# Hybrid DeltaNet and window-attention layer, one core: SiLU gate on ACT, decays computed one supertile ahead, another PSUM split, triangle DMAs in four pieces

## Chip, cores and metric

The kernel runs on one core of a Trainium2 chip. The metric is the device time of one execution in microseconds (us); smaller is better. Engines are named as in the profile: PE multiplies matrices, DVE, ACT and POOL work on vectors, SP issues most DMAs. Each engine takes its instructions strictly in the order in which they were written into its stream.

## What is computed

One layer of a decoder step for a prompt of 4096 tokens (width 1024) and 8 single-token samples. Float32 throughout in the reference:

```python
h = x * (1 + scale) + shift
proj = h @ w_in
qkv, new_conv = causal_conv(conv_buf, proj[..., 0:1536], conv_w)      # 4 taps, then silu
qa = l2_normalize(qa) * 128 ** -0.5 ; ka = l2_normalize(ka)           # 4 heads of 128
beta = sigmoid(proj_beta)
g = -exp(a_log) * softplus(proj_decay + dt_bias)
# gated delta rule: S_t = exp(g_t) (I - b_t k_t k_t^T) S_{t-1} + b_t k_t v_t^T ; o_t = S_t^T q_t
oa = rms_norm(o, norm_a) * silu(za)
ob = window_attention(rotary(qb), rotary(kb), vb, sinks) * silu(zb)   # window 128
y = layer_norm(alpha * x + (1 + gate) * (concat(oa, ob) @ w_out))
```

Outputs are y for prompt and samples and the new convolution, delta and window states.

## The kernel before

The program has three stages. Stage 1 (to about 1200 us) computes the delta-rule branch for the prompt and, piece by piece, side work (weight splits for later stages, the samples' delta step). Stage 2 (to about 1600 us) is the window attention. Stage 3 is the gate and output projections with layer norm. The change touches stage 1 only, and of the later stages nothing.

Stage 1 loops over 16 **supertiles** `s` of 256 tokens, each two chunks `c` of 128, four heads each, so eight (chunk, head) pairs `m`. A supertile passes through:

- `xt`: modulated input `hT` in two float16 halves, written by ACT (L253, L255) and DVE (L256). It is made one supertile ahead, by `ahead()` in the middle of `front`.
- `front`, decays: eight small projections into `bd`, then beta (Tanh, L273) and `g` by `softplus_ops` (an Exp and a chain of DVE instructions, L105), split into `g16`. Later in `front` PE sums `g16` along the chunk (`tr<-g,c`, `pga<-c,g`), and ACT takes exponentials: `G` (L333), the 128x128 decay matrices `dec` (L348), the last column `eGl` (L349).
- `front`, `group`: channels of keys, queries and values, 24 matmuls of 128x256 for each 128 channels (`pj<-hT,w`), an eviction (`u`, L309, and L313), three more convolution taps on DVE (L315), then the gate. With `th = tanh(x/2)` from ACT (L321) DVE forms `(th+1)*x` (L322), which is twice SiLU. L2 norms, `Kd`, `Vn` and the constants 4e-6 and 0.25 allow for that factor.
- `front`, products: keys, queries and values are transposed through a PSUM bank called `tr` (L355, L389, L399). `pga<-kqv` gives k.k and q.k; DVE makes the triangular `U` (L379) and `Aqk` (L382).
- `lanes`: the eight 128x128 triangles' four diagonal 32x32 blocks are inverted on DVE. `U`'s blocks go to DRAM (L411, four DMAs), come back as `LU` (one DMA that repeats the 128 KB four times along the partitions), 31 steps of two DVE instructions each (L420, L422) build `LV`, which goes to DRAM in one DMA (L424) and comes back as `VTd` in four (L429).
- `gdn_inv`: from `VTd` and `U16` the whole inverse, for each chunk a chain PE, ACT, DVE, PE with small operands (L433 to L480). `gdn_c`: the recurrence through the state `S` (L491 `r`, L503 `ut`, L508 `S`).

PSUM has eight banks: `pga` 1, `xt` 1, `tr` 1, `pj` 2, `pgi` 3. The `xt` bank serves the side work.

The order in which each engine takes its work is set when the program is built: a scheduler of the tile framework moves instructions of different steps and supertiles between each other. So the inverse of one supertile lies between the products of the next, and the 62 steps on `LV` lie between convolution taps.

```python
LU = w1p.tile([128, 32, 32], F32, name="LU", bufs=1)
sp.dma_start(LU.rearrange("p a b -> p (a b)"), d1[None].to_broadcast([4, 32, 1024]))
...
d2w = d2.rearrange("l (j c i) -> c l j i", c=4, i=32)
sp.dma_start(d2w, LV)
```

Of the kernel before, what the change touches and what calls it, by code (L numbers as in the profile page):

```python
# [9 lines left out]
F32 = mybir.dt.float32  # L10
# [23 lines left out]
def body(ctx, tc, I, O, seq):  # L34
# [5 lines left out]
    def mm(out, l, r, st=True, sp_=True):  # L40
        pe.matmul(out, l, r, start=st, stop=sp_)  # L41
# [69 lines left out]
    with ExitStack() as p1:  # L111
# [5 lines left out]
        wk = p1.enter_context(tc.tile_pool(name="wk", bufs=2))  # L117
        sml = p1.enter_context(tc.tile_pool(name="sml", bufs=2))
        pga = p1.enter_context(tc.tile_pool(name="pga", bufs=1, space=PSUM))
        pxt = p1.enter_context(tc.tile_pool(name="pxt", bufs=1, space=PSUM))  # L120
        pst = p1.enter_context(tc.tile_pool(name="pst", bufs=1, space=PSUM))
        pj = p1.enter_context(tc.tile_pool(name="pj", bufs=2, space=PSUM))
        pgi = p1.enter_context(tc.tile_pool(name="pgi", bufs=3, space=PSUM))

        def tr_ps(shape, dt=F32):
            return pst.tile(shape, dt, name="tr")

        def xt_ps(shape, dt=F32):
            return pxt.tile(shape, dt, name="xt")

        def load_x(s):

            xs = []
            for q in range(2):
                x = wf.tile([128, 4, 256], F32, name="x", bufs=3)
                sp.dma_start(x, I["xT"][s][:, 4 * q:4 * q + 4])
                xs.append(x)
            return xs
# [88 lines left out]
        def load_bd():  # L227
            sp.dma_start(wbd32, I["wbd"])
            split(wbd[:, :, 0:8], wbd[:, :, 8:16], wbd32)
# [27 lines left out]
            sp.dma_start(hD[s], hT.rearrange("p a k t -> p (a k t)"))  # L257
            return hT

        def front(s, hT, ahead):  # L260

            bd = tr_ps([128, 2, 16])
            for c in range(2):
# [5 lines left out]
            act.activation(bdS, bd, AF.Copy, scale=IWS)  # L269
            x8 = sml.tile([128, 2, 8], F32, name="x8")  # L270
            dve.tensor_add(x8, bdS[:, :, 0:8], bdS[:, :, 8:16])
            be = sml.tile([128, 2, 4], F32, name="be")
            act.activation(be, x8[:, :, 0:4], AF.Tanh, scale=0.5)  # L273
            dve.tensor_scalar(be, be, 1.0, 0.5, op0=ALU.add, op1=ALU.mult)
            xd = sml.tile([128, 2, 4], F32, name="xd")
# [2 lines left out]
            softplus_ops(sml, xd, g, [128, 2, 4], "sp")  # L278
            dve.tensor_mul(g, g, nega[:, None, :].to_broadcast([128, 2, 4]))
            dve.tensor_scalar(g, g, -30000.0, None, op0=ALU.max)  # L280
            g16 = sml.tile([128, 2, 8], F16, name="g16")
            gf = g.rearrange("p a b -> p (a b)")
            dve.tensor_copy(g16[:, 0], gf)
            dve.tensor_sub(g16[:, 1], gf, g16[:, 0])
            kqv = wk.tile([128, 8, 256], F32, name="kqv", bufs=2)
            vv = wf.tile([128, 4, 256], F32, name="vv", bufs=1)
            U = wk.tile([128, 8, 128], F32, name="U", bufs=1)
# [2 lines left out]
            Kd = wk.tile([128, 8, 128], F32, name="Kd", bufs=2)  # L290
            Vn = wk.tile([128, 8, 128], F32, name="Vn", bufs=2)
            sse = sml.tile([128, 2, 8], F32, name="sse")
            sc = sml.tile([128, 6, 8], F32, name="sc")
            junk = wf.tile([128, 128], F32, name="junk", bufs=1)

            def group(grp, dst):
                for pr in range(2):
                    b0 = grp * 4 + pr * 2
                    u = wf.tile([128, 2, 259], F32, name="u", bufs=3)
                    pool.tensor_copy(u[:, :, 0:3], hist[:, b0:b0 + 2, :])  # L300
                    ps = pj.tile([128, 2, 256], F32, name="pj")
                    for b2 in range(2):
                        n = 0
                        w = w1[b0 + b2]
                        for k in range(8):
                            for wi, hi in ((0, 0), (0, 1), (1, 0)):
                                mm(ps[:, b2, :], w[:, wi, k, :], hT[:, hi, k, :], n == 0, n == 23)
                                n += 1
                    act.activation(u[:, :, 3:259], ps, AF.Copy, scale=IWS)  # L309
                    for b2 in range(2):  # L310
                        blk = b0 + b2
                        d = dst[:, pr * 2 + b2, :]
                        act.activation(d, ps[:, b2, :], AF.Copy, scale=cw64[:, blk:blk + 1])  # L313
                        for j in range(3):
                            dve.scalar_tensor_tensor(d, u[:, b2, j:j + 256], cwj(j, blk), d,  # L315
                                                     op0=ALU.mult, op1=ALU.add)
                    pool.tensor_copy(hist[:, b0:b0 + 2, :], u[:, :, 256:259])
                    if pr == 0:
                        yield
                th = wf.tile([128, 4, 256], F32, name="th", bufs=1)  # L320
                act.activation(th, dst, AF.Tanh, scale=0.5)  # L321
                dve.scalar_tensor_tensor(dst, th, 1.0, dst, op0=ALU.add, op1=ALU.mult)  # L322


            keys, qrs, vls = group(1, kqv[:, 4:8]), group(0, kqv[:, 0:4]), group(2, vv)
            next(keys)
            next(keys, None)
            next(qrs)
            ps = tr_ps([128, 8])
            mm(ps, triU, g16[:, 0], True, False)  # L330
            mm(ps, triU, g16[:, 1], False, True)
            G = sml.tile([128, 4, 8], F32, name="G")
            act.activation(G[:, 0], ps, AF.Exp)  # L333
            act.activation(G[:, 1], ps, AF.Copy, scale=-1.0)
            dve.tensor_scalar(G[:, 2], G[:, 0], -1.0, None, op0=ALU.mult)
            eGl = sml.tile([128, 2, 4], F32, name="eGl")
            decs = []
            for c in range(2):
                dec = wf.tile([128, 4, 128], F32, name="dec", bufs=2)
                pg = pga.tile([128, 4, 128], F32, name="pga")  # L340
                for h in range(4):
                    m = 4 * c + h
                    mm(pg[:, h, :], idb, negm, True, False)
                    mm(pg[:, h, :], g16[:, 0, m:m + 1].to_broadcast([128, 128]), triU, False, False)
                    mm(pg[:, h, :], g16[:, 1, m:m + 1].to_broadcast([128, 128]), triU, False, True)
                for h in range(4):
                    m = 4 * c + h
                    act.activation(dec[:, h, :], pg[:, h, :], AF.Exp, bias=G[:, 1, m:m + 1])  # L348
                act.activation(eGl[:, c, :], pg[:, :, 127], AF.Exp)  # L349
                decs.append(dec)  # L350

            for c in range(2):
                pk = tr_ps([128, 4, 128])
                for h in range(4):
# [1 line left out]
                for h in range(4):  # L356
                    m = 4 * c + h
                    act.activation(junk, pk[:, h, :], AF.Square, accum_out=sse[:, 1, m:m + 1])
                    act.activation(Kd[:, m, :], pk[:, h, :], AF.Copy, scale=decs[c][:, h, 127:128])
            dve.tensor_scalar(sse[:, 1], sse[:, 1], 4e-6, None, op0=ALU.add)  # L360
            dve.tensor_scalar(sc[:, 5], sse[:, 1], 0.25, None, op0=ALU.mult)
            pool.tensor_tensor(sc[:, 0], sc[:, 5], half_pos[:, 0:8], op=ALU.pow)
            dve.reciprocal(sc[:, 1], sse[:, 1])
            dve.tensor_mul(sc[:, 2], be.rearrange("p a b -> p (a b)"), sc[:, 1])
            dve.tensor_scalar(sc[:, 3], sc[:, 2], -1.0, None, op0=ALU.mult)
# [20 lines left out]
            for c in range(2):  # L386
# [3 lines left out]
                for h in range(4):  # L390
                    m = 4 * c + h
                    act.activation(junk, pq[:, h, :], AF.Square, accum_out=sse[:, 0, m:m + 1])
            dve.tensor_scalar(sc[:, 4], sse[:, 0], 4e-6, 1.28e-4, op0=ALU.add, op1=ALU.mult)

            next(vls, None)
            for c in range(2):
                pv = tr_ps([128, 4, 128])
                for h in range(4):
                    pe.transpose(pv[:, h, :], vv[:, h, c * 128:(c + 1) * 128], ident)  # L399
                for h in range(4):  # L400
                    m = 4 * c + h
                    act.activation(Vn[:, m, :], pv[:, h, :], AF.Copy, scale=sc[:, 0, m:m + 1])
            return kqv, G, sc, U16, Aqk, Kd, Vn, eGl, vt, vt16

        def lanes(s, U):
# [4 lines left out]
                bs = slice(32 * b, 32 * b + 32)  # L410
                sp.dma_start(d1v[b], U[bs, :, bs])  # L411
            LU = w1p.tile([128, 32, 32], F32, name="LU", bufs=1)
            sp.dma_start(LU.rearrange("p a b -> p (a b)"), d1[None].to_broadcast([4, 32, 1024]))
            LV = w1p.tile([128, 8, 32], F32, name="LV", bufs=1)
            dve.tensor_copy(LV.rearrange("p a b -> p (a b)"), lv0)
            lt = w1p.tile([128, 8, 32], F32, name="lt", bufs=1)
# [4 lines left out]
                               LU[:, None, 0:j, j].to_broadcast([128, n, j]))  # L421
                dve.tensor_add(LV[:, j0:, 0:j], LV[:, j0:, 0:j], lt[:, j0:, 0:j])  # L422
            d2w = d2.rearrange("l (j c i) -> c l j i", c=4, i=32)
            sp.dma_start(d2w, LV)  # L424
            d2r = d2.rearrange("(m b) (q i) -> b q m i", b=4, i=32)
            vt = VTd
            for b in range(4):
# [269 lines left out]
        wst = [fetch_w1(g) for g in range(4, 8)]  # L697
        nxt = [xt(0, xs, True)]
        load_bd()
        for g in (4, 5, 6, 7):  # L700
            split_w1(g, wst[g - 4])
        for g in (0, 1, 2, 3, 8, 9, 10, 11):
# [3 lines left out]

        def ahead(s):
            if s < NS:
                nxt[0] = xt(s, load_x(s))

        for s in range(NS):
            kqv, G, sc, U16, Aqk, Kd, Vn, eGl, vt, vt16 = front(s, nxt[0], lambda: ahead(s + 1))
            Vs = [gdn_inv(c, U16, vt, vt16) for c in range(2)]
            for c in range(2):
                gdn_c(s, c, kqv, G, sc, Aqk, Kd, Vn, eGl, Vs[c])
            for side in sides:
                next(side, None)
# [737 lines left out]
```

## Time and profile before

| what | value |
|---|---|
| median of 3 runs | 2308.78 us (2307.01 to 2318.52) |
| the profiled execution, its own time | 2309.84 us |
| its span in the profile | 2308.1 us |
| PE busy | 2119.3 us, 92% |
| DVE busy | 1834.1 us, 79% |
| ACT busy | 1266.6 us, 55% |
| POOL busy | 162.0 us, 7% |
| DMA | 232.18 MB, 101 GB/s over the span |

A busy share is an average over stages with different limits. An engine's wait is put down to the instruction or DMA whose event came last. The span is measured inside the profile; the execution's own time is 1.7 us more.

### The profile page before, as it was taken

Reading aid. Unit: us, or ns where it says so; the run is one execution under the profiler, and the core shown is the slowest. Engines: PE = TensorE matmul, PEld = TensorE weight load, DVE = VectorE, ACT = ScalarE, POOL = GpSimd, SP = SyncE. Lnnn points to the kernel's source line nnn. Section 1 sums busy time; section 2 is a strip of 40 time slices with the busy share of each in tenths; the row PEclk is TensorE's granted clock in tenths of the full one; section 3 lists DMA queues with packets and bytes.
Section 4 is the critical chain, followed back from the end, with each engine's and each line's share of the span. In section 5 each row is a group of like instructions: output and inputs, shape, how many; then the busy total and the mean of one; then the engine's idle time right before and its main releaser. Section 6 shows DMA issues by size and latency. Waiting matters only on the chain.

```text
span 2308.1 us, 48753 instructions
## 1 busy us (share of the span) xinstructions
PE 2119.3 (92%) x18287; PEld 1516.0 (66%) x18287; DVE 1834.1 (79%) x5546; ACT 1266.6 (55%) x3601; POOL 162.0 (7%) x284
## 2 busy tenths in 40 slices
PE   6988798898989898899899999999999999999997
PEld 4867677787877787787576777777545454444443
DVE  7778677888888788888767977777687788898877
ACT  6755656666666576666455666666632333434332
POOL 1111110111111011110000000000000000000000
PEclk9999999999999999999899999999999999999999
DMA  8332322323333123222334311111342343333322
GB/s 321 117 114 67 88 88 72 101 89 94 124 101 98 60 76 99 77 67 79 97 102 165 113 59 63 58 59 39 125 169 74 115 141 105 115 106 111 108 91 74
DMA packets 139757, 232.18 MB, mean 101 GB/s; under 512 B 60933, under 2 KB 73529, under 8 KB 133353
## 3 DMA queue, kind: packets, MB, share of 16 engines
q1 hardware_dynamic: 138224, 228.52, 29.5%
q8 instruction: 144, 2.36, 0.4%
q14 instruction: 93, 0.75, 0.1%
q10 hardware_dynamic: 1296, 0.55, 0.1%
HBM read 154.07 MB, written 76.09 MB: 100 GB/s over the span
## 4 chain that ended last, share of the span: by engine, by line
PE 42%; DVE 17%; DMA 7%; ACT 6%; issue 2%; SPq 1%; POOL 0%; POOLq 0%; ACTq 0%; DVEq 0%
PE pp L1040 21%; PE pj L41 9%; DMA LU<-D 3%; PE pgi L41 3%; DVE kqv L315 2%; ACT Sm L870 2%; PE po L41 2%; DVE lt L420 2%; PE tr L887 2%; DVE LV L422 1%; PE tr L41 1%; PE pS L41 1%; DMA D<-LV 1%; DVE bst L1075 1%; PE pga L41 1%
## 5 line engine op out<-in xcount | busy, mean ns | idle before, releaser
L41 PE MATMUL pj<-hT,w 128*128 128x256 f16 x4608 | 578.8, 276 | 3.4 <-ACT hT L255 2.6
L41 PEld LDWEIGHTS <-w 128*128 128x128 f16 x4800 | 452.8, 99 | 62.2 <-issue 6.8
L1040 PEld LDWEIGHTS <-S 128*128 128x128 f16 x1536 | 150.4, 99 | 170.7 <-issue 3.6
L41 PEld LDWEIGHTS <-hT 128*128 128x128 f16 x2048 | 159.8, 98 | 69.3 <-issue 2.0
L41 PE MATMUL pj<-wq,hT 128*128 128x512 f16 x768 | 191.8, 379 | 0.0
L315 DVE SCALAR_TENSOR_TENSOR kqv<-u,cols,kqv 128x256 f32<-128x256 f32 x384 | 181.4, 478 | 2.7 <-ACT kqv L313 2.1
L1040 PE MATMUL pp<-wz,S 128*128 128x512 f16 x768 | 181.1, 382 | 0.0
L870 ACT ACTIVATE Sm<-Sm,nm 128x256 f32<-128x256 f32 (+1 forms) x256 | 125.5, 492 | 92.4 <-DVE nm L867 92.3
L1040 PE MATMUL pp<-wo,S 128*128 128x512 f16 x768 | 171.3, 379 | 0.7 <-DVE zs L1216 0.6
L420 DVE TENSOR_TENSOR lt<-LV,LU 128x60 f32<-128x60 f32 (+24 forms) x496 | 119.4, 241 | 54.9 <-DMA LU<-D 48.8
L1040 PE MATMUL pp<-wz,hT 128*128 128x512 f16 x576 | 133.0, 382 | 1.2 <-ACT zs L1127 1.2
L863 DVE CUSTOM_DVE_ANT_0 Sm<-pS,swam 128x256 f32<-128x256 f32 (+1 forms) x256 | 96.4, 415 | 35.5 <-PE tr L887 32.0
L1040 PE MATMUL pp<-wo,A 128*128 128x512 f16 x540 | 122.1, 379 | 0.0
L41 PE MATMUL pj<-wkv,hT 128*128 128x256 f16 x768 | 107.7, 275 | 0.4 <-ACT v L814 0.4
L1040 PEld LDWEIGHTS <-hT 128*128 128x128 f16 x612 | 60.1, 99 | 72.7 <-issue 4.4
L422 DVE TENSOR_TENSOR LV<-LV,lt 128x60 f32<-128x60 f32 (+24 forms) x496 | 102.6, 207 | 6.2
L41 PE MATMUL pga<-kqv 128*128 128x256 f32 x256 | 75.3, 409 | 25.7 <-DVE kqv L322 25.7
L1079 POOL TENSOR_TENSOR rs<-rs,cf 128x1 f32<-128x1 f32 (+1 forms) x33 | 22.8, 692 | 1077.1 <-DVE rs L1078 1077.1
L1040 PEld LDWEIGHTS <-A 128*128 128x128 f16 x540 | 52.9, 99 | 62.0
L1021 ACT ACTIVATE S<-zt 128x512 f16<-128x512 f32 x64 | 40.2, 630 | 85.3 <-DVE zt L1027 81.1
L1134 ACT ACTIVATE zs<-zs 128x512 f32<-128x512 f32 x48 | 30.2, 629 | 100.5 <-DVE zs L1133 100.5
L315 DVE SCALAR_TENSOR_TENSOR vv<-u,cols,vv 128x256 f32<-128x256 f32 x192 | 82.6, 479 | 1.7 <-ACT vv L313 0.9
(378 smaller groups left out, 4607.0 us busy)
## 6 DMA issues: line engine op xcount, KB each, us to landing
hT<-hD SPq DMA_DIRECT2D x32, 1024.0 KB
x<-in_xT_dram SPq DMA_DIRECT2D x32, 512.0 KB
hD<-hT SPq DMA_DIRECT2D x16, 1024.0 KB
x<-in_x_prompt_dram SPq DMA_DIRECT2D x60, 256.0 KB
out_y_prompt_dram<-x SPq DMA_DIRECT2D x60, 256.0 KB
stg<-in_ws_dram SPq DMA_DIRECT2D x16, 512.0 KB
LU<-D SPq DMA_DIRECT2D x16, 512.0 KB
wS<-wt SPq DMA_DIRECT2D x16, 512.0 KB
```

Source lines behind the costliest of these rows:

```text
L41: pe.matmul(out, l, r, start=st, stop=sp_)
L315: dve.scalar_tensor_tensor(d, u[:, b2, j:j + 256], cwj(j, blk), d, op0=ALU.mult, op1=ALU.add)
L420: dve.tensor_mul(lt[:, j0:, 0:j], LV[:, j0:, j:j + 1].to_broadcast([128, n, j]), LU[:, None, 0:j, j].to_broadcast([128, n, j]))
L422: dve.tensor_add(LV[:, j0:, 0:j], LV[:, j0:, 0:j], lt[:, j0:, 0:j])
L863: dve.tensor_tensor_reduce(Sm[:, h, k0:256], pS[:, h2, k0:256], swam[:, k0:256], 0.125, -1e30, op0=ALU.add, op1=ALU.max, accum_out=mx[:, h ...
L870: act.activation(Sm[:, h, k0:256], Sm[:, h, k0:256], AF.Exp, bias=nm[:, h:h + 1], accum_out=sm_[:, h:h + 1])
L887: pe.transpose(pt[:, h2, kb, :], Sm[:, h + h2, kb * 128:(kb + 1) * 128], ident)
L1021: act.activation(q[:, 0], src, AF.Copy)
L1040: pe.matmul(dst.rearrange("p (u c) -> p u c", c=128), A[:, hi, k, :], W[:, k // 2::2, q, wi, k % 2, :], start=new and n == 0, stop=n == 11 ...
L1075: dve.bn_stats(st[0:n, q, :], r[q][0:n])
L1079: pool.tensor_tensor(rs[0:n, 1:2], rs[0:n, 0:1], half_neg[0:n, 0:1], op=ALU.pow)
L1134: act.activation(zs, zs, AF.Silu, scale=IWS)
```

## The change

Five edits, all in stage 1.

1. The gate of the channels is one ACT instruction, `Silu`, in place of Tanh on ACT and a multiply on DVE. The factor of two goes, and with it the constants for it (one small DVE instruction less per supertile).
2. Everything that depends on the decays alone moves into a function `decays(hT)`, which is called a supertile ahead, at the end of `front`; `G`, `be`, `g16`, `eGl` get three buffers and `dec` four.
3. Ordering edges without a semaphore keep the exponentials and the gates of ACT apart: a gate comes behind the last exponential written before it, an exponential behind the last gate. (The Exp inside `softplus_ops` and Tanh have no such edge.)
4. The `xt` bank is given up. The side work shares the `tr` bank, and the projections' pool `pj` has three banks.
5. In `lanes` the load of `LU` and the store of `LV` are four DMAs of 32 partitions each.

```diff
-        pxt = p1.enter_context(tc.tile_pool(name="pxt", bufs=1, space=PSUM))
-        pj = p1.enter_context(tc.tile_pool(name="pj", bufs=2, space=PSUM))
+        pj = p1.enter_context(tc.tile_pool(name="pj", bufs=3, space=PSUM))
...
         def xt_ps(shape, dt=F32):
-            return pxt.tile(shape, dt, name="xt")
+            return pst.tile(shape, dt, name="tr")
...
+        def after_exps(i):
+            if "exp" in order:
+                tc.add_manual_dep(i.ins, order["exp"].name, NOSYNC, reason="gates after exponentials")
+            order["gate"] = i.ins
+        def after_gates(i):
+            if "gate" in order:
+                tc.add_manual_dep(i.ins, order["gate"].name, NOSYNC, reason="exponentials after gates")
+            order["exp"] = i.ins
+        def decays(hT):
...
+            after_gates(act.activation(G[:, 0], ps, AF.Exp))
...
+                dec = wf.tile([128, 4, 128], F32, name="dec", bufs=4)
...
+                    after_gates(act.activation(dec[:, h, :], pg[:, h, :], AF.Exp, bias=G[:, 1, m:m + 1]))
+                after_gates(act.activation(eGl[:, c, :], pg[:, :, 127], AF.Exp))
+                decs.append(dec)
+            return be, g16, G, eGl, decs
+        def front(s, hT, dcy, ahead):
+            be, g16, G, eGl, decs = dcy
...
-                th = wf.tile([128, 4, 256], F32, name="th", bufs=1)
-                act.activation(th, dst, AF.Tanh, scale=0.5)
-                dve.scalar_tensor_tensor(dst, th, 1.0, dst, op0=ALU.add, op1=ALU.mult)
+                after_exps(act.activation(dst, dst, AF.Silu))
...
+            if s + 1 < NS:
+                nxt.append(decays(nxt[0]))
             return kqv, G, sc, U16, Aqk, Kd, Vn, eGl, vt, vt16
...
-            sp.dma_start(LU.rearrange("p a b -> p (a b)"), d1[None].to_broadcast([4, 32, 1024]))
+            for c in range(4):
+                sp.dma_start(LU[32 * c:32 * c + 32].rearrange("p a b -> p (a b)"), d1)
...
-            sp.dma_start(d2w, LV)
+            for c in range(4):
+                sp.dma_start(d2w[c], LV[32 * c:32 * c + 32])
```

The edits move instructions on every engine. Three places matter below; names end in numbers that the build gives them.

**DVE, from a supertile's inverse to the first step on `LV`** (lines ahead of the change; `lt<-LV,LU 128x31` is the first instruction that needs the loaded `LU`):

```order
L322 SCALAR_TENSOR_TENSOR vv<-th,vv 128x1024
L466 COPY V<-pgi 32x4x32
L467 COPY V<-pgi 32x4x32
L678 SCALAR_TENSOR_TENSOR stg<-xt,dkq,stg 128x128
L256 TENSOR_TENSOR hT<-x,hT 128x512
L451 TENSOR_TENSOR VR<-V,VR 64x256
L256 TENSOR_TENSOR hT<-x,hT 128x512
L451 TENSOR_TENSOR V_319<-pgi,V_319 64x256
L420 TENSOR_TENSOR lt<-LV,LU 128x31
```

The same place in the changed kernel, where the inverse's lines are L469 to L485:

```order
L469 TENSOR_TENSOR V_316<-pgi,V_316 64x256
L304 TENSOR_SCALAR G<-G 128x8
L684 TENSOR_TENSOR dt_9737<-tr,deg 128x4
L685 SCALAR_TENSOR_TENSOR ddl<-dy,dt_9737 128x4
L686 TENSOR_TENSOR ddl<-ddl,dbe 128x4
L687 TENSOR_TENSOR dt_9737<-tr,deg 128x4
L688 TENSOR_TENSOR doT<-ddl,dqk 128x4
L689 TENSOR_TENSOR doT<-doT,dt_9737 128x4
L469 TENSOR_TENSOR XZ<-pgi,XZ 64x4x64
L399 TENSOR_TENSOR U_8786<-U,U_8786 128x1024
L509 SCALAR_TENSOR_TENSOR r<-pgi,G,Vn 128x128 x4
L437 TENSOR_TENSOR lt<-LV,LU 128x31
```

Before, the first step on `LV` stood ahead of the end of the second chunk's inverse. Now the whole inverse of both chunks, the second half of the decays (`G`), the split of `U` and the recurrence's first instruction `r` stand ahead of it.

**PE, where the decays are summed.** Before, they stand among the projections (`pj<-hT,w_3` are key or query channels of the same supertile):

```order
L41 MATMUL pj<-hT,w_2_381 128x256
L41 LDWEIGHTS w_3_386
L41 MATMUL pj<-hT,w_3_386 128x256
L41 LDWEIGHTS c_63
L41 MATMUL tr<-g_9748,c_63 128x8
L41 LDWEIGHTS g_9748
L41 MATMUL pga<-c_63,g_9748 128x128
L41 LDWEIGHTS cb
L41 MATMUL pga<-cb 128x128
```

In the changed kernel (L489 transposes the inverse so far, `V`):

```order
L42 LDWEIGHTS w_7_473
L42 MATMUL pj<-hT,w_7_473 128x256
L489 MATMUL pgi<-cf,V 128x128 x4
L42 LDWEIGHTS c_63
L42 MATMUL tr<-g_9424,c_63 128x8
L42 LDWEIGHTS g_9424
L42 MATMUL pga<-c_63,g_9424 128x128
```

The decays' matmuls of the next supertile now lie inside the inverse of the second chunk.

**ACT, a gate and the exponentials.** Before, the gate's Tanh (`th`) is followed at once by the exponentials of the same supertile:

```order
L321 ACTIVATE th<-kqv 128x1024
L313 ACTIVATE kqv<-pj,cw_77 128x256 x2
L333 ACTIVATE G<-tr 128x8
L334 ACTIVATE G<-tr 128x8
L348 ACTIVATE dec<-pga,G 128x128 x4
L349 ACTIVATE eGl<-pga 128x4
```

In the changed kernel the exponentials lie in the inverse (L468, L474, L498), and a table load stands ahead of them:

```order
L468 ACTIVATE XZ<-pgi 64x4x64
L102 ACT_TABLE_LOAD
L102 ACTIVATE spu<-spab 128x8
L498 ACTIVATE V<-pgi 64x4x64
L474 ACTIVATE V<-pgi 128x512
L468 ACTIVATE XE<-pgi 128x8x32
L468 ACTIVATE Vo<-V 128x256
```

There are 38 `ACT_TABLE_LOAD` in the changed program and 4 in the one before; 17 of the 34 new ones stand ahead of a gate, 17 ahead of an exponential of a softplus. Each waits for nothing itself; the semaphore wait is on the instruction behind it.

## Rows read from the trace of the kernel before

**Rows 1.** Windows: stretch, length, busy us (count) PE PEld DVE ACT POOL, clock, DMA share, GB/s.
```profile
50.00:1200.00 1150.00, 1020.92 (x9971) 875.38 (x9969) 934.54 (x3232) 718.55 (x2307) 133.79 (x238) 0.96 0.29 90
1200.00:1600.00 400.00, 388.96 (x4378) 282.11 (x4377) 307.50 (x1163) 244.53 (x747) 1.12 (x1) 1.00 0.24 89
```
**Rows 2.** One line's instructions: the first ACT work on each supertile's decays.
```profile
L269 ACT ACTIVATE bdS<-tr x16: 175/197/221, 48.1 to 1074.9; 128x32 f32<-128x32 f32 x16
```
**Rows 3.** PE's waits, 50 to 1160 us: for what, us in total, times, longest.
```profile
PE pga L41 <- DVE kqv L322: 25.7, 16, 3.6
PE tr L41 <- DVE g L283: 19.9, 13, 2.0
...
PE tr L389 <- ACT junk L392: 2.7, 10, 0.3
...
PE pj L41 <- ACT kqv L313: 0.2, 1, 0.2
```
**Rows 4.** The chain that ended last, pieces of one supertile: start, us, what.
```profile
858.49 9.41 DMA LU<-D
...
897.20 1.13 DVE kqv L322
...
906.67 4.74 DMA D<-LV
...
928.05 1.65 DMA D<-U
```
**Rows 5.** DVE's waits, 50 to 1160 us.
```profile
DVE lt L420 <- DMA LU<-D: 48.8, 14, 7.3
...
DVE LV L415 <- DMA D<-LV: 11.4, 5, 3.2
```
**Rows 6.** Windows as in rows 1, 2 us inside a load of `LU`.
```profile
995.00:997.00 2.00, 1.94 (x22) 1.53 (x21) 1.94 (x6) 1.40 (x3) 0.00 (x0) 1.00 0.23 76
```
**Rows 7.** Timeline of SP's DMA queue: start, us of the issue, DMA.
```profile
647.65 1.78 SPq L411 DMA_DIRECT2D D<-U  x4
650.65 0.55 SPq L413 DMA_DIRECT2D LU<-D  x1
```
**Rows 8.** Groups of instructions: line, engine, shape, count, busy us, mean ns, idle before.
```profile
L322 DVE SCALAR_TENSOR_TENSOR kqv<-th,kqv 128x1024 f32<-128x1024 f32 x32 | 39.0, 1219 | 8.4 <-ACT th L321 8.4
L322 DVE SCALAR_TENSOR_TENSOR vv<-th,vv 128x1024 f32<-128x1024 f32 x16 | 19.5, 1222 | 1.0 <-ACT th L321 0.8
L1134 ACT ACTIVATE zs<-zs 128x512 f32<-128x512 f32 x48 | 30.2, 629 | 100.5 <-DVE zs L1133 100.5
```
**Rows 9.** Timeline of ACT around one of the four table loads.
```profile
1632.71 1.05 ACT L890 ACTIVATE PT<-tr 128x512 f16<-128x512 f32 x2
1633.78 1.28 ACT L1134 ACT_TABLE_LOAD   x1
1635.07 0.63 ACT L1134 ACTIVATE zs<-zs 128x512 f32<-128x512 f32 x1
```
**Rows 10.** ACT's wait ahead of the gate, 50 to 1160 us.
```profile
ACT th L321 <- DVE kqv L315: 51.5, 24, 4.8
```
**Rows 11.** Timeline of DVE: first and last instruction of one supertile's inverse.
```profile
572.33 0.69 DVE L433 TENSOR_TENSOR vt<-VTd,vt 128x512 f16<-128x512 f32 x1 [1.29 <-ACT vt L432]
...
589.06 1.13 DVE L491 SCALAR_TENSOR_TENSOR r<-pgi,G,Vn 128x128 f32<-128x128 f32 x4
```
**Rows 12.** Groups of instructions, as in rows 8: pieces of the decays.
```profile
L348 ACT ACTIVATE dec<-pga,G 128x128 f32<-128x128 f32 x128 | 37.4, 395 | 6.1 <-PE pga L41 6.0
L41 PE MATMUL pga<-c,g 128*128 128x128 f16 x256 | 28.0, 223 | 0.0
L41 PE MATMUL pga<-cb 128*128 128x128 bf16 x128 | 24.6, 224 | 0.8 <-ACT eGl L349 0.2
L105 DVE SCALAR_TENSOR_TENSOR spp<-spp,spu 128x8 f32<-128x8 f32 x144 | 22.9, 159 | 0.3
L41 PE MATMUL tr<-wbd,hT 128*128 128x8 f16 (+1 forms) x512 | 16.8, 169 | 0.1
```

More of the change, by code (lines that the diff above doesn't have):

```diff
@@ L18 @@
 D = 1024
+NOSYNC = mybir.DependencyInfo(mybir.DependencyClass.NoSync, mybir.DependencyReason.DATA)
 OFF_AZ = 1536
@@ L258, in xt @@
             return hT
-        def front(s, hT, ahead):
+        order = {}
+        def after_exps(i):
[7 more added lines that the diff above has]
+        def decays(hT):
             bd = tr_ps([128, 2, 16])
@@ L271, in front @@
             dve.tensor_add(x8, bdS[:, :, 0:8], bdS[:, :, 8:16])
-            be = sml.tile([128, 2, 4], F32, name="be")
+            be = sml.tile([128, 2, 4], F32, name="be", bufs=3)
             act.activation(be, x8[:, :, 0:4], AF.Tanh, scale=0.5)
@@ L280, in front @@
             dve.tensor_scalar(g, g, -30000.0, None, op0=ALU.max)
-            g16 = sml.tile([128, 2, 8], F16, name="g16")
+            g16 = sml.tile([128, 2, 8], F16, name="g16", bufs=3)
             gf = g.rearrange("p a b -> p (a b)")
@@ L284, in front @@
             dve.tensor_sub(g16[:, 1], gf, g16[:, 0])
+            ps = tr_ps([128, 8])
+            mm(ps, triU, g16[:, 0], True, False)
+            mm(ps, triU, g16[:, 1], False, True)
+            G = sml.tile([128, 4, 8], F32, name="G", bufs=3)
+            after_gates(act.activation(G[:, 0], ps, AF.Exp))
+            act.activation(G[:, 1], ps, AF.Copy, scale=-1.0)
+            dve.tensor_scalar(G[:, 2], G[:, 0], -1.0, None, op0=ALU.mult)
+            eGl = sml.tile([128, 2, 4], F32, name="eGl", bufs=3)
+            decs = []
+            for c in range(2):
+                dec = wf.tile([128, 4, 128], F32, name="dec", bufs=4)
+                pg = pga.tile([128, 4, 128], F32, name="pga")
+                for h in range(4):
+                    m = 4 * c + h
+                    mm(pg[:, h, :], idb, negm, True, False)
+                    mm(pg[:, h, :], g16[:, 0, m:m + 1].to_broadcast([128, 128]), triU, False, False)
+                    mm(pg[:, h, :], g16[:, 1, m:m + 1].to_broadcast([128, 128]), triU, False, True)
+                for h in range(4):
+                    m = 4 * c + h
+                    after_gates(act.activation(dec[:, h, :], pg[:, h, :], AF.Exp, bias=G[:, 1, m:m + 1]))
[4 more added lines that the diff above has]
+            be, g16, G, eGl, decs = dcy
             kqv = wk.tile([128, 8, 256], F32, name="kqv", bufs=2)
@@ L292, in front @@
             sse = sml.tile([128, 2, 8], F32, name="sse")
-            sc = sml.tile([128, 6, 8], F32, name="sc")
+            sc = sml.tile([128, 5, 8], F32, name="sc")
             junk = wf.tile([128, 128], F32, name="junk", bufs=1)
@@ L328, in front @@
             next(qrs)
[L329 to L350, printed above, removed]
             for c in range(2):
@@ L359, in front @@
                     act.activation(Kd[:, m, :], pk[:, h, :], AF.Copy, scale=decs[c][:, h, 127:128])
-            dve.tensor_scalar(sse[:, 1], sse[:, 1], 4e-6, None, op0=ALU.add)
-            dve.tensor_scalar(sc[:, 5], sse[:, 1], 0.25, None, op0=ALU.mult)
-            pool.tensor_tensor(sc[:, 0], sc[:, 5], half_pos[:, 0:8], op=ALU.pow)
+            dve.tensor_scalar(sse[:, 1], sse[:, 1], 1e-6, None, op0=ALU.add)
+            pool.tensor_tensor(sc[:, 0], sse[:, 1], half_pos[:, 0:8], op=ALU.pow)
             dve.reciprocal(sc[:, 1], sse[:, 1])
@@ L392, in front @@
                     act.activation(junk, pq[:, h, :], AF.Square, accum_out=sse[:, 0, m:m + 1])
-            dve.tensor_scalar(sc[:, 4], sse[:, 0], 4e-6, 1.28e-4, op0=ALU.add, op1=ALU.mult)
+            dve.tensor_scalar(sc[:, 4], sse[:, 0], 1e-6, 1.28e-4, op0=ALU.add, op1=ALU.mult)
             next(vls, None)
@@ L699, in body @@
         load_bd()
+        nxt.append(decays(nxt[0]))
         for g in (4, 5, 6, 7):
@@ L708, in ahead @@
             if s < NS:
-                nxt[0] = xt(s, load_x(s))
+                nxt[:] = [xt(s, load_x(s))]
         for s in range(NS):
-            kqv, G, sc, U16, Aqk, Kd, Vn, eGl, vt, vt16 = front(s, nxt[0], lambda: ahead(s + 1))
+            kqv, G, sc, U16, Aqk, Kd, Vn, eGl, vt, vt16 = front(s, *nxt, lambda: ahead(s + 1))
             Vs = [gdn_inv(c, U16, vt, vt16) for c in range(2)]
```

## The prediction

> **What bounds the kernel now.** I began with the windows by stage [rows 1]. In stage 1, 50 to 1200 us, PE is busy 1020.9 of 1150 us (89%), in stage 2 it is busy 389.0 of 400 (97%). So stage 1 holds 129 us of idle PE, and the change touches only that stage. Sixteen supertiles run in it; the first work on their decays starts at 48.1 and 1074.9 us [rows 2], so one supertile takes (1074.9 - 48.1) / 15 = 68.5 us. PE has 1020.9 / 1150 x 68.5 = 60.8 us of work in each, and waits 7.7.
>
> Then the waits: what PE waits for most is DVE. It waits 25.7 us for the gated keys and queries and 19.9 us for the decays `g` [rows 3]. DVE itself is busy 934.5 of 1150 us [rows 1], 55.6 us in a supertile: it is neither full nor free, and it is late because it stands still at certain places. Two of them are DMAs: 48.8 us for the load of `LU` (14 times, 3.5 us each, 7.3 at most) and 11.4 us for the store of `LV` [rows 5].
>
> The chain of waits shows the loop [rows 4]. In one supertile it runs: load of `LU` (9.41 us), recurrence and DVE's long stretch with the 62 steps on `LV` among convolution taps, in which one gate multiply lies (1.13 us), store of `LV` (4.74 us), inverse and products, `U`'s blocks to DRAM (1.65 us), and the next load of `LU`. Behind a stalled DVE stand the taps, the gates, `r` and `g`, for which PE waits.
>
> **The change part by part.**
>
> *The DMAs in four.* While a load of `LU` runs and little else moves, the 16 DMA engines are busy 23% of the time at 76 GB/s [rows 6]: about a quarter of them works. The load is described as four repeats of 32 rows, the store as four groups `c`; both have four as their outermost dimension. Each new piece has 32 partitions, as `U`'s blocks have. If the pieces use all engines, the data need 9.41 x 0.25 = 2.4 us. Four issues took 1.78 us on SP's queue, against 0.55 for the one [rows 7]. So `LU` lands about 4.2 us after its first issue instead of 9.4, and `LV` after 1.78 + 1.65 = 3.4 (from the last of `U`'s four blocks [rows 4]) instead of 4.7. Six further issues per supertile, 6 x 0.45 = 2.7 us, lie on SP's queue; behind them stand stores and prefetches, which nobody waits for within 3 us. The 5.2 us that `LU` gains exceed the mean wait of 3.5. Also, DVE's order now puts the whole inverse of both chunks ahead of the first step on `LU`. I take both waits as gone: -48.8 and -11.4 us. Ends: 0, if another wait follows at the same place, and these sums.
>
> The Trainium skill says in "DMA: Bandwidth & Descriptors", section "Why a DMA increments its semaphore by 16 and not by 1", that a DMA is split over the largest number of engines up to 16 that divides the outermost dimension of both sides. By that rule the four-fold ones get 4 engines, with which the 23% agree, and the pieces of 32 get 16.
>
> *The gate.* 48 DVE multiplies of 1.22 us go: 39.0 us for keys and queries, 19.5 for values [rows 8]. Silu takes Tanh's place on ACT at the same shape; ACT's function does not set its time (Silu 0.63 us at 128x512 [rows 8], the evictions of that shape 1.05 us for two [rows 9]). The tap-to-PE path gets shorter by the multiply, and DVE gets free. The gates of keys and queries lie in DVE's long stretch and on the chain; the values' gate lies near the wait for `LU`. I take -39.0; ends 0 and -58.5.
>
> *Table loads.* The program has 34 more, 17 ahead of gates and 17 ahead of softplus exponentials. One takes 1.28 us: ACT ends an eviction at 1633.76, loads from 1633.78, and the Silu starts at 1635.07 [rows 9]. Those ahead of a gate are hidden: they wait for nothing, and ACT waits there for DVE's taps, 51.5 us in 24 waits, 2.1 each [rows 10]. Without that wait they would cost as much as the others. Those ahead of an exponential stand inside the inverse, where ACT's next instruction is a link of the chain: 17 x 1.28 = 21.8 us, half of it exposed, since ACT often waits there as well. +10.9 us; ends 0 and 43.5.
>
> *The decays a supertile ahead.* No work goes or comes but the loads. PE's 19.9 us of waiting for `g` go with the place, not into the sum, as they were a consequence of the late DVE. What matters is the new place: the inverse, 572.3 to 589.1 us in one supertile, 17 us [rows 11], in which PE, ACT and DVE wait for each other in turn. The pieces that come between, per supertile: ACT 37.4 / 16 = 2.3 for `dec`, about 1.4 for the small ones and 1.3 for the load, 5.0 in all; PE (28.0 + 24.6 + 16.8) / 16 = 4.3; DVE 22.9 / 16 = 1.4 and as much for its smaller ones, 3.0 [rows 12]. In series 12.3 us, beside other work 0. As each engine idles in about half of those 17 us, I take 1.0 us: +16 us; ends 0 and 197.
>
> *The banks.* PE waited 0.2 us in all for a projection bank [rows 3], so the third bank alone is worth nothing I can see; I cost it at 0 to -0.2. The side work's 43 tiles now share `tr`. A handover of `tr` to PE costs 2.7 us in 10 waits, 0.27 each [rows 3]: +11.6 us; ends 0 and 45 (two evictions, 1.05 us [rows 9], each time). The ordering edges of exponentials and gates have no wait of their own; ACT's order is already in the order from which I argue. The one small DVE instruction less is nothing.
>
> **Sum:** -48.8 - 11.4 - 39.0 + 10.9 + 16 + 11.6 = -60.7 us on the profiled execution of 2309.8, which lies 1 us above the median of the runs: **2249 us**. Check by the supertile: 68.5 - 60.7 / 16 = 64.7 us against 60.8 of PE work, PE busy 94%, still below stage 2's 97%.
>
> **Rivals.**
>
> *Everything is gained.* The values' gate counts too, and nothing that is added is exposed: -48.8 - 11.4 - 58.5 = -118.7, 2191 us. For it: PE's idle time, 129 us, would allow it. Against: PE would be busy 99%. Chance 0.12.
>
> *The DMAs do not do what they say.* The pieces queue behind each other on the same quarter of the engines, or the place of the DMA wait is taken by another (the store of `LV`, `VTd`). Then -39.0 + 38.5 is left, 2309 us, from 2295 to 2320. For it: no row shows a piece of 128 KB. Against: `U`'s pieces of 32 partitions land in 1.65 us. Chance 0.12.
>
> *A switch of tables costs more than its load.* After a load ACT would stand still, and all 17 loads in the inverse would be exposed: +34 us, 2283. The rows show nothing of it: 0.02 us ahead of the load, none behind [rows 9]. Chance 0.07. The Trainium skill speaks against the change here: "ScalarE: Activation LUTs", section "What ACT_TABLE_LOAD costs", gives 1.28 us for the load and 1.38 us more for a drain, 2.66 us for each switch. By that page 17 exposed switches are an estimated 45 us instead of my 10.9; the trace agrees with its first figure and shows no second.
>
> *The inverse gets longer: slower than before.* The decays' pieces join the inverse's links in series. If all 12.3 us do, the supertile takes 11.3 more than in my sum: 2249 + 181 = 2430 us. The point from which it decides: 60.7 / 16 = 3.8 us above my 1.0, so 4.8 us in all bring back 2310; ACT's part alone is 5.0. For it: each engine takes its order strictly, and PE's decay matmuls wait for a DVE chain of some 20 instructions. Against: PE waited less than 2 us for that chain even while DVE was late. Chance 0.09.
>
> **How the numbers follow.** My forecast, 2225 to 2275, has 0.60; with the rivals' 0.12, 0.12, 0.07 and 0.09 that is 1. A difference of 0.5%, 11.5 us, is about what a measurement of this kernel can tell from no change. Faster by more: 0.60 + 0.12 + 0.07 and a quarter of the second rival, 0.82; within: 0.08; slower: 0.09 and the tail of the second, 0.10. The range, 2200 to 2308 us, leaves out the slower case, some of the second rival and the best of the first, 0.19 in all.
>
> **What would show it.** Right: the load of `LU` lands 4 to 5 us after its first issue at a DMA share well above a quarter; DVE's wait for it falls from 48.8 us to below 10; PE's busy share in stage 1 rises to about 94%; DVE has some 58 us less work; 17 table loads of 1.28 us stand in the inverse. Wrong: `LU` still takes 9 us; or the stretch from `vt` to `r` grows from 17 us to 22 or more; or PE shows new waits of tens of us for `tr`, for `g` or for the gates. If DVE's waits go and the supertile still takes 68 us, then the links of the inverse were the bound and not the DMAs.

## The result and the profile after

| what | before | after |
|---|---|---|
| median of 4 runs | 2309.13 us | 2240.28 us (2239.1 to 2243.7) |
| ratio, 95% interval | | 0.9697 [0.9668, 0.9725] |
| the profiled execution's span | 2308.1 us | 2241.9 us (its own time 2243.7) |
| PE busy | 2119.3 us, 92% | 2109.0 us, 94% |
| DVE busy | 1834.1 us | 1780.0 us |
| ACT busy | 1266.6 us | 1305.5 us |

The change makes the kernel about 3% faster, 69 us by the medians. The windows of the changed kernel, each stage moved forward by some 70 us (columns as in [rows 1]):

```profile
50.00:1130.00 1080.00, 1011.05 (x9975) 859.91 (x9974) 879.28 (x3168) 756.18 (x2335) 139.31 (x238) 0.98 0.30 97
```

PE is busy 1011.05 / 1080 = 93.6% of stage 1, against 89% in [rows 1], at a granted clock of 0.98 instead of 0.96. DVE's `vt`, the start of the inverse, comes once in each supertile and so gives the period. The line of `vt` before the change:

```profile
L433 DVE TENSOR_TENSOR vt<-VTd,vt x16: 682/692/693, 157.3 to 1165.1; 128x512 f16<-128x512 f32 x16
```

and after it:

```profile
L451 DVE TENSOR_TENSOR vt<-VTd,vt x16: 681/692/694, 164.1 to 1103.9; 128x512 f16<-128x512 f32 x16
```

Fifteen periods of (1165.1 - 157.3) / 15 = 67.19 us have become 62.65. So the span can be split without rest: 6.8 us more to the first `vt`, 15 x 4.54 = 68 less in the loop, 5 less from the last `vt` to the end, -66.2 in all. The loop is the whole gain.

DVE's waits from 50 to 1100 us in the changed kernel, where `lt` and the store of `LV` stood first in [rows 5]:

```profile
DVE vt L451 <- ACT vt L450: 15.8, 11, 3.6
DVE spp L104 <- ACT spu L102: 14.6, 14, 1.6
...
DVE x L284 <- ACT bdS L282: 12.1, 6, 4.4
DVE gateT L174 <- PE tr L42: 12.0, 8, 2.1
```

No DMA of the triangles is among them any more. The new ones are small pieces: ACT's answers inside the inverse and the decays, and `gateT`, side work that waits for the shared bank. PE's waits, against [rows 3]:

```profile
PE pga L42 <- ACT kqv L360: 10.4, 15, 1.8
...
PE tr L42 <- DVE g L296: 3.1, 7, 0.9
```

The wait for the gated keys and queries fell from 25.7 to 10.4 us, the one for `g` from 19.9 to 3.1. The load of `LU` itself, four issues on SP's queue (timeline: start, us of the issues):

```profile
420.81 1.84 SPq L430 DMA_DIRECT2D LU<-D  x4
```

and windows over it, in which the DMA share and GB/s are the last two columns:

```profile
420.80:422.00 1.20, 1.17 (x40) 1.07 (x39) 0.57 (x2) 1.20 (x4) 0.19 (x1) 1.00 1.19 423
422.00:423.00 1.00, 1.00 (x20) 0.95 (x17) 0.30 (x1) 0.92 (x4) 0.00 (x0) 1.00 0.72 266
423.00:424.00 1.00, 0.97 (x11) 0.73 (x9) 0.81 (x5) 1.00 (x4) 0.00 (x0) 1.00 0.75 189
424.00:425.00 1.00, 1.00 (x19) 0.84 (x17) 0.31 (x2) 0.98 (x2) 0.00 (x0) 1.00 0.29 102
425.00:426.00 1.00, 1.00 (x10) 0.71 (x8) 0.08 (x1) 0.96 (x3) 0.00 (x0) 1.00 0.07 16
```

All is moved after some 4.5 us, at shares of 0.7 and more while the bulk of it runs, where one DMA held 0.23 and 76 GB/s for 9.4 us [rows 4, 6]. (The first window holds the end of another store as well.) ACT around a table load in the inverse:

```profile
740.37 0.21 ACT L286 ACTIVATE be<-x 128x8 f32<-128x8 f32 x1 [0.52 <-DVE x L284]
740.59 1.28 ACT L102 ACT_TABLE_LOAD   x1
741.89 0.21 ACT L102 ACTIVATE spu<-spab 128x8 f32<-128x8 f32 x1
742.12 0.41 ACT L468 ACTIVATE VR<-V 64x256 f16<-64x256 f32 x1
```

The load takes 1.28 us and the exponential starts 0.02 us behind it, as in [rows 9]. Behind the exponential stands `VR`, a link of the inverse.

### The profile page after: what moved, and what is told of

The parts are those of the page before. It is cut to its first block, busy times and chain, and to the rows that moved or that the text cites. A ratio compares the mean times of both kernels' runs of the same rounds, so it can differ in the third digit from the quotient of the medians.

```text
span 2241.9 us, 48847 instructions
## 1 busy us (share of the span) xinstructions
PE 2109.0 (94%) x18287; PEld 1499.5 (67%) x18287; DVE 1780.0 (79%) x5482; ACT 1305.5 (58%) x3635; POOL 167.4 (7%) x284
## 4 chain that ended last, share of the span: by engine, by line
PE 44%; DVE 13%; ACT 6%; issue 2%; DMA 2%; POOL 1%; POOLq 0%; SPq 0%; DVEq 0%; ACTq 0%
PE pp L1059 21%; PE pj L42 10%; PE pgi L42 3%; ACT Sm L889 2%; PE po L42 2%; PE tr L42 2%; PE tr L906 2%; DVE kqv L355 1%; PE pS L42 1%; DVE bst L1094 1%; DVE lt L437 1%; DVE LV L439 1%; DVE x L1102 1%; DVE vv L355 1%; DMA dw<-in_wdec_dram 1%
## 5 line engine op out<-in xcount | busy, mean ns | idle before, releaser
L42 PE MATMUL pj<-hT,w 128*128 128x256 f16 x4608 | 571.8, 274 | 3.9 <-ACT hT L255 2.6
L42 PE MATMUL pga<-kqv 128*128 128x256 f32 x256 | 70.7, 399 | 26.4 <-ACT kqv L360 10.4
L355 DVE SCALAR_TENSOR_TENSOR vv<-u,cols,vv 128x256 f32<-128x256 f32 x192 | 88.9, 480 | 8.1 <-ACT vv L353 8.1
```

## The experiments

Each ratio is to the kernel before on the same chip. Where two variants are compared, I turn the difference of their ratios into us of 2309.

**The DMAs undone in the changed kernel.**

```diff
-            for c in range(4):
-                sp.dma_start(LU[32 * c:32 * c + 32].rearrange("p a b -> p (a b)"), d1)
+            sp.dma_start(LU.rearrange("p a b -> p (a b)"), d1[None].to_broadcast([4, 32, 1024]))
...
-            for c in range(4):
-                sp.dma_start(d2w[c], LV[32 * c:32 * c + 32])
+            sp.dma_start(d2w, LV)
```

> The changed kernel with the load of LU and the store of LV as one DMA each again. Theory A (the four-fold DMAs ran on a quarter of the DMA engines, and DVE's stand-still behind them set the period of the supertile): LU again takes 9 to 10 us at a DMA share of 0.23 to 0.27, DVE waits for it 40 to 60 us in stage 1 and 5 to 15 us more behind the store, PE's busy share there falls back to 90 or 91%, and the time is 2285 to 2300 us. Rival B (the gain is the DVE work that the gate lost; the load was covered by other DVE work once DVE had less to do): 2240 to 2255 us, DVE's wait for LU below 15 us.

Measured: 2345.08 us, ratio 1.0125 [1.0093, 1.0156]. It is slower than the kernel before, outside both expectations on theory A's side. DVE's waits, 50 to 1100 us:

```profile
DVE lt L436 <- DMA LU<-D: 60.3, 14, 6.5
DVE LV L431 <- DMA D<-LV: 23.6, 12, 4.2
```

Rival B falls. DVE has lost the multiplies of the gate, yet it stands 84 us at the load and at the store, against 57 in the same stretch of the kernel before (60 in [rows 5], which reach to 1160 us). That it arrives there earlier is my reading and not shown. What the waits do show is that PE waits 34.3 us for `g`, where the kernel before has 19.9 and the changed one 3.1: the next supertile's decays now stand on DVE behind the first steps on `LU`. Next to the rest of the change the pieces are worth 1.0125 - 0.9697, 99 us.

**The DMAs alone, on the kernel before.** The opposite edit, in `before`.

> The kernel before with only the two DMAs in four pieces of 32 partitions. Theory A: LU lands in 4 to 5 us from its first issue, DVE's waits of 48.8 and 11.4 us go, the time is 2250 to 2265 us. Rival B (another link of DVE's chain, the gates and the decays, takes the place of the wait): 2295 to 2310 us. Rival C (each half of the change needs the other): e1 and e2 each gain little, their gains add up to less than half of the 69 us.

Measured: 2235.26 us, ratio 0.9651 [0.962, 0.9681]. This is more than theory A expected, and it alone accounts for the whole gain of the change (0.9697). DVE's wait for `LU` is gone. PE's waits, 50 to 1100 us:

```profile
PE pga L41 <- DVE kqv L322: 24.0, 16, 2.3
PE tr L41 <- DVE g L283: 12.0, 9, 3.5
```

PE still waits 24 us for the gate's multiply, which Silu would shorten, and the kernel is no slower than the changed one for it.

**`LU` in two DMAs of 64 partitions.**

```diff
-            for c in range(4):
-                sp.dma_start(LU[32 * c:32 * c + 32].rearrange("p a b -> p (a b)"), d1)
+            for c in range(2):
+                sp.dma_start(LU[64 * c:64 * c + 64].rearrange("p a b -> p (a b)"), d1[None].to_broadcast([2, 32, 1024]))
```

> The changed kernel with the load of LU in two DMAs of 64 partitions, each with two repeats as its outermost dimension; the store of LV stays in four. Theory A1 (a DMA uses as many engines as its outermost dimension has entries, here 2): a DMA share of about 0.12 if both DMAs fall on the same two engines, or 0.25 on four, LU lands in 9 to 19 us, the time is 2285 us or more. Theory A2 (more DMAs in flight help, whatever their shape): LU lands in 5 to 6 us at a share of 0.5, the time stays below 2260 us.

Measured: 2368.12 us, ratio 1.0222 [1.0185, 1.0259], and DVE waits 95.3 us for `LU` in 50 to 1100. Windows over the start and the end of one load, whose two DMAs were issued from 678.40 to 679.52 us:

```profile
680.00:682.00 2.00, 2.00 (x20) 1.93 (x19) 1.63 (x5) 1.23 (x5) 0.76 (x1) 1.00 0.09 31
...
690.00:692.00 2.00, 2.00 (x21) 1.79 (x20) 0.00 (x0) 0.00 (x0) 0.00 (x0) 1.00 0.38 94
692.00:694.00 2.00, 1.47 (x14) 1.08 (x11) 0.00 (x0) 0.00 (x0) 0.00 (x0) 1.00 0.13 53
694.00:696.00 2.00, 0.00 (x0) 0.00 (x0) 1.74 (x13) 1.52 (x3) 0.00 (x0) 1.00 0.13 55
696.00:698.00 2.00, 0.00 (x0) 0.00 (x0) 1.79 (x12) 2.00 (x6) 1.26 (x2) 0.87 0.12 49
698.00:700.00 2.00, 0.00 (x0) 0.00 (x0) 2.00 (x13) 1.73 (x4) 0.00 (x0) 0.50 0.05 20
```

and DVE's first step on it:

```profile
694.12 0.21 DVE L437 TENSOR_TENSOR lt<-LV,LU 128x31 f32<-128x31 f32 x1 [8.78 <-DMA LU<-D]
```

It is 15.7 us from the issue to the step. Where the load runs alone, with both DMAs issued, the share is 0.09 at its start and 0.13 at its end (692 to 694 us): 2 of 16 engines, both DMAs on the same two. (What still runs at 0.13 behind 694.12 us are other transfers.) A1 holds, with its lowest share; A2 falls. It is the outermost dimension that decides, not the number of DMAs: four repeats 0.23, two repeats 0.13, 32 partitions 0.7 and more. (The last rows also show PE idle and its granted clock going to 0.50; more of this below.) The Trainium skill's rule in "DMA: Bandwidth & Descriptors", "Why a DMA increments its semaphore by 16 and not by 1", that a DMA uses the largest number of engines up to 16 that divides the outermost dimension of both sides, agrees with all three.

**Tanh and the multiply back in the changed kernel.**

```diff
-                after_exps(act.activation(dst, dst, AF.Silu))
+                th = wf.tile([128, 4, 256], F32, name="th", bufs=1)
+                act.activation(th, dst, AF.Tanh, scale=0.5)
+                dve.scalar_tensor_tensor(dst, th, 1.0, dst, op0=ALU.add, op1=ALU.mult)
```

> The changed kernel with the gate as before: Tanh on ACT and a multiply on DVE, with its constants; the 34 table loads go with it. My terms: 39.0 us for the multiplies come back, 10.9 us of table loads go, so 28 us more than the changed kernel, 2268 us. Theory D (DVE's work is on the path in full, the loads are hidden): 2280 to 2300 us. Rival E (with the DMA waits gone DVE has room and PE is the bound): 2235 to 2250 us.

Measured: 2286.94 us, ratio 0.9873 [0.9846, 0.99]; theory D's range, 41 us above the changed kernel. So decays ahead and shared bank, without Silu, cost 51 us against the DMAs alone. The next four runs looked for which.

**The old banks in the changed kernel.** `xt` has its bank again, `pj` two.

> The changed kernel with the bank for the side work back and two banks for projections. The first four runs say that the change without its DMAs costs about 26 us and the DMAs alone gain about 80, so something in the rest of the change costs some 50 us, which the gate pays back. Theory G (the side work on the bank of the transposes is what costs): 2190 to 2210 us, DVE's wait of 12 us for gateT goes. Theory F (the decays inside the inverse cost it): within 10 us of the changed kernel, 2230 to 2250 us. My term was 11.6 us for the shared bank: 2229 us.

Measured: 2234.5 us, ratio 0.9643 [0.961, 0.9675]: 12 us below the changed kernel, the size of my own term. The time lies in F's range and well above G's.

**The decays in their own supertile, all else as changed.**

```diff
-            be, g16, G, eGl, decs = dcy
+            be, g16, G, eGl, decs = decays(hT)
```

> The changed kernel with the decays computed in their own supertile, as the first step of front, all else kept. Theory F (the decays between the links of the inverse cost some 50 us): 2190 to 2215 us, the mean stretch from vt to r shrinks. Theory G (it is the shared bank): 2235 to 2250 us. A third way, H: the decays were moved for a reason, PE again waits 20 to 40 us for g at the front's start, and the time is 2255 to 2290 us.

Measured: 2252.72 us, ratio 0.9723 [0.9685, 0.9761]: 6 us above the changed kernel, within the intervals, and between G and H. F falls: taking the decays out of the inverse gains nothing. PE's wait for `g` is 15.1 us instead of 3.1. The mean stretch from `vt` to `r` is 18.5 us, in the changed kernel 17.9, before 19.1 (means of 13 supertiles): it didn't lengthen by the decays.

**The DMAs and the decays, without Silu and with the old banks.**

> The kernel before with the DMAs in four and the decays a supertile ahead, but with Tanh and the multiply for the gate and the old banks; it differs from the kernel before with the four-piece DMAs alone by the place of the decays. Theory F: 2270 to 2290 us. Theory G: 2230 to 2245 us. By my own sum the decays cost 16 us: 2251 us.

Measured: 2244.16 us, ratio 0.9678 [0.9647, 0.9709]: G's range, 6 us above the DMAs alone, and the intervals overlap.

**The DMAs and the banks alone.**

> The kernel before with the DMAs in four and the new split of the banks, nothing else; it differs from the kernel before with the four-piece DMAs alone by the banks. Theory G: 2270 to 2290 us, with new waits for tr. Theory F: 2230 to 2245 us. By my own sum the shared bank costs 11.6 us: 2247 us.

Measured: 2262.39 us, ratio 0.9759 [0.9728, 0.979], 25 us above the DMAs alone, clear of its interval. DVE's first wait:

```profile
DVE gateT L173 <- PE tr L41: 18.7, 8, 5.9
```

In the kernel with the DMAs alone, which has the old banks, the same wait reads:

```profile
DVE gateT L174 <- PE xt L41: 2.7, 3, 1.1
```

Here the shared bank costs more than I had put down, less than theory G wanted. So neither F nor G explains the 51 us alone: 25 come with the bank, and the decays add 26 on top of it (0.9759 to 0.9873), though by themselves they cost 6. Why the two cost more together than apart, no run shows.

**`LU` alone in pieces, on the kernel before.** The store of `LV` stays one DMA.

> The kernel before with the load of LU alone in four pieces; the store of LV stays one DMA. Both in pieces gave 2235 us, 75 to 80 us less. Theory A (each wait counts for itself, as in my sum): 48.8 of 60.2 parts of that gain, 2245 to 2255 us, DVE waits 10 to 30 us behind the store. Theory A3 (the load alone is the loop; the store's wait is absorbed by taps): 2235 to 2242 us. Theory A4 (the whole loop of one supertile is a chain, and the store's 4.8 us lie on it in full): 2265 us or more.

Measured: 2236.51 us, ratio 0.9665 [0.964, 0.969]; theory A3. DVE waits 4.2 us behind the store in 50 to 1100 us. The load alone is worth 77 us, the store nothing that can be measured.

**The changed kernel with the old banks and the decays in their own supertile.** The edits of two runs above together: DMAs, Silu and its edges remain, and the decays are computed at the start of `front`.

> The changed kernel with the decays in their own supertile, at the start of front, and the old banks; DMAs in four, Silu and its 34 table loads remain. Theory P (with the DMAs in pieces PE's own work is the bound of stage 1, and the rest of the change neither gains nor costs there): 2230 to 2245 us, a supertile of 62.4 to 63.0 us. Theory S (Silu is a gain of its own of 10 us or more once the decays are left where they were): 2215 to 2225 us.

Measured: 2235.86 us, ratio 0.967 [0.9641, 0.9698], a supertile of 62.43 us; theory P's numbers.

**Tanh in Silu's place, no multiply, old banks.**

```diff
-                after_exps(act.activation(dst, dst, AF.Silu))
+                after_exps(act.activation(dst, dst, AF.Tanh, scale=0.5))
```

> The changed kernel with the old banks, and Tanh in place where Silu stood: neither the multiplies on DVE nor the table loads, so the gate is not SiLU. It differs from the kernel with the old banks and Silu (2234.5 us) by 34 table loads, and from the one with Tanh, multiply and old banks (2244 us) by 48 multiplies. Theory P: 2228 to 2236 us, as the loads and the multiplies both lie beside PE's work. My terms: the loads cost 10.9 us, so 2224 us. The page's price of 2.66 us for a switch: 2190 us.

Measured: 2231.18 us, ratio 0.9645 [0.9618, 0.9673] against 0.9643 with Silu. The 34 loads that are gone are 4.5 us by the spans of one execution each (2231.9 to 2227.4), nothing by the ratios, whose intervals leave room for some 9 us. The time lies in theory P's range.

**A part of PE's work left out, old banks.** The expectation names the part, so this kernel does not compute the full product.

```diff
-                            for wi, hi in ((0, 0), (0, 1), (1, 0)):
+                            for wi, hi in ((0, 0), (0, 1), (1, 0))[:3 - grp // 2]:
```

> The changed kernel with the old banks and 512 of 6144 projection matmuls left out (the values' products of the low weight part with the high input part), 3.4 us of PE work at 107 ns each in a supertile of 62.5. Theory P (PE is the bound of stage 1 now): 2180 to 2195 us, a supertile of 59 to 60 us. Rival L (the loop of DVE, ACT and DMA links from U to the next U is the bound, PE only happens to be nearly full): 2220 to 2236 us, a supertile above 61.5 us, and new waits of PE.

Measured: 2219.1 us, ratio 0.9588 [0.9561, 0.9614], 13 us below the kernel with the old banks by the ratios, and a supertile of 61.40 us instead of 62.49. That is 1 us outside rival L's range and 24 us above theory P's. In the profiled executions PE's busy time fell by 33.4 us (2095.2 to 2061.8) and the span by 20.6, but this one's own time, 2213.14 us, lies 6 us below the median. The windows, first of the kernel with the old banks:

```profile
50.00:1080.00 1030.00, 961.84 (x9631) 829.21 (x9629) 867.14 (x3071) 739.28 (x2262) 114.31 (x236) 0.99 0.32 99
```

then with less PE work:

```profile
50.00:1080.00 1030.00, 945.59 (x9285) 805.48 (x9284) 866.50 (x3133) 744.94 (x2305) 141.14 (x237) 0.97 0.31 100
```

With more room PE is busy 92% instead of 93%, its clock falls from 0.99 to 0.97, and the mean matmul (of all shapes) takes 101.8 ns instead of 99.9. In windows of 1 us from 50 to 1100, PE worked 57 us at a mean clock under 0.75, against 20 in the kernel with the old banks. PE has a new wait, 9.6 us for `r` in 17 times. So PE is not the bound alone. Of 3.4 us of work taken from each supertile 1.1 came out, since the loop through DVE and ACT lies close behind, and part of what was taken came back as a slower clock.

## Why the prediction was right

Forecast and result agree: 2249 us, measured 2240. The cause that the prediction put first, a load of `LU` on a quarter of the DMA engines, is the one that the runs show. That the sum came within 9 us is partly luck, since its terms miss by 50 us one way and 41 the other.

**The load of `LU`** was given 48.8 us; alone it is worth 77 (0.9665). What my term left out was PE's clock. In the spans, 2308.1 against 2235.0, the 73.1 us consist of 49.0 us less idle PE (188.8 to 139.8, span less busy time), almost my number (though mine was a wait of DVE), and 24.1 us less busy PE (2119.3 to 2095.2) for the same 18287 matmuls. One stall of the kernel before shows how. DVE:

```profile
247.00 0.21 DVE L420 TENSOR_TENSOR lt<-LV,LU 128x31 f32<-128x31 f32 x1 [7.26 <-DMA LU<-D]
...
250.36 1.12 DVE L491 SCALAR_TENSOR_TENSOR r<-pgi,G,Vn 128x128 f32<-128x128 f32 x4
```

PE:

```profile
250.76 0.80 PE L41 MATMUL pgi<-r,V 128*128 128x128 f32 x2 [8.58 <-DVE r L491]
```

and the windows (PE's busy time first, the granted clock third from the end):

```profile
244.00:246.00 2.00, 0.00 (x0) 0.00 (x0) 0.00 (x0) 0.00 (x0) 0.00 (x0) 0.69 0.62 164
246.00:248.00 2.00, 0.00 (x0) 0.00 (x0) 0.87 (x5) 0.01 (x1) 0.00 (x0) 0.50 0.25 96
...
250.00:252.00 2.00, 1.24 (x6) 1.12 (x7) 1.66 (x8) 2.00 (x10) 1.01 (x1) 0.50 0.04 16
252.00:254.00 2.00, 2.00 (x11) 1.81 (x10) 0.87 (x3) 1.29 (x4) 0.00 (x0) 0.50 0.00 0
254.00:256.00 2.00, 2.00 (x15) 1.88 (x14) 1.33 (x5) 1.21 (x5) 0.00 (x0) 0.75 0.00 0
256.00:258.00 2.00, 2.00 (x45) 1.95 (x44) 1.84 (x7) 1.66 (x5) 0.00 (x0) 1.00 0.00 0
```

`r` is queued on DVE behind the first steps that wait for `LU` (and, for the last 1.5 us, behind one that waits for ACT); PE stands 8.58 us for `r`, the clock falls to 0.50 (1.2 GHz), and when work comes again PE does the first 4 to 5 us of it at half speed. The four transposes `tr<-cf,vv` take 1.06 us at 253.70 us, at 0.50, and 0.60 us at 599.85 us, at 1.00. Summed over windows of 1 us from 50 to 1100, PE worked 69 us at a mean clock under 0.75 before, 40 after, and 25 in the kernel with the DMAs alone. An estimate from the same windows, each one's busy time multiplied by the part of the clock that was not granted, gives 35.2 us lost before and 11.2 with `LU` alone in pieces. The difference, 24.0 us, agrees with the 24.1 us of busy time.

**The store of `LV`**, -11.4: this step failed. With `LU` in pieces and the store as it was, the wait is 4.2 us, and taking it away gains nothing measurable. The two waits were not independent.

**The gate**, -39.0: Silu takes ACT 1.06 us at 128x1024, as Tanh did, which I had assumed. In the change as it stands the gate is worth about my term, -41 us (run with Tanh and shared bank). But with the old banks it is -8 us with overlapping intervals, and +4 where the decays stay in their own supertile (0.9651 to 0.967). So the multiplies counted next to the shared bank and hardly without it; that PE's own work covers them there is my reading.

**Table loads**, +10.9: 4.5 us by the spans, nothing by the ratios, with room for some 9. The rival by which a switch costs more than its load falls: the exponential starts 0.02 us behind the load, and even 9 us for all 34 is less than the 21.8 us of 17 loads alone. The Trainium skill, "ScalarE: Activation LUTs", section "What ACT_TABLE_LOAD costs", has 1.38 us more for a drain; the trace agrees with its 1.28 us for the load and shows no drain.

**The decays**, +16: in three of four pairs of kernels that differ by their place, +6, -6 and -6 us, inside the intervals. In the fourth, Tanh with the shared bank, +26. The stretch from `vt` to `r` didn't grow (there it is 17.6 us on the mean), so the rival of a longer inverse falls, and in those three pairs my 1.0 us per supertile was too much; PE's wait for `g`, which I left out of the sum as a consequence, was not worth anything measurable either.

**The banks**, +11.6: this holds in size, 12 us with Silu in two pairs (the intervals overlap a little), 25 and 45 without it (they don't). Its place is only partly what I said. With Silu and the decays ahead, 8.2 of the 10.0 us of span come before the first `vt` (155.9 to 164.1) and not from a handover in each supertile; in three of the four pairs the first `vt` is 7.5 to 8.7 us later. Why the first supertile is later, and why the bank costs more without Silu, stays open.

Laid out one after another in ratios: `LU` -77, `LV` -3, gate with its loads +4, decays ahead -6, banks +12, in all -70; in another order the gate and the decays get other shares. My sum had -60.7. It gave `LU` 28 us too little and charged the decays 22 us that they don't cost; against that stand gains in the gate with its loads (32) and the store (8) that aren't there. One reading was off as well: the period of 68.5 us counts from decays that start well ahead of the loop, and `vt` gives 67.19.

**The rivals.** That the DMAs don't do it falls with the first two runs. That everything is gained (2191 us) fails on what five kernels show, with DMAs alone, with Silu, with the decays ahead, with neither multiply nor table loads: all end between 2231 and 2237 us with a supertile of 62.1 to 63.2. There PE is busy 92 to 93% from 50 to 1080 us, and work taken from DVE or ACT moves nothing that can be measured. The version with the old banks (0.9643) is the best of those that keep the rest of the change, and no run tells it apart from the kernel before with the DMAs alone.

## What to carry to other kernels

Before splitting, moving or shortening vector work, look for DMAs whose outermost dimension is small: the DMA share in a window where one runs alone shows it (0.23 here), and the remedy is a description with many partitions outermost, not simply more DMAs. Price a stall that reaches PE at its idle time and also at the slower matmuls behind it. And price the terms of a change again after each one: once the one stall was gone and the old banks were kept, neither the multiplies nor the table loads were worth their busy time, while next to the shared bank the multiplies were worth 41 us.

## What the runs showed of the hardware

I had left open where two small DMAs in flight go. With two repeats outermost both ran at a share of 0.13 in all and took 15.7 us, where one DMA with four repeats took 10.3 (673.08 us in the chain of the changed kernel with the DMAs undone): the share is that of two engines in all and not of two each. What I had not expected is that a third of what a DMA wait cost (24 of 73 us) would stand in PE's busy time and not in anyone's waits.
